# Stationary weights by chunk: all high products, then all low ones, with the low buffers moved in SBUF

## The chip, the core and the metric

The kernel runs on one core of a Trainium2 chip. The metric is the device time of one execution in microseconds (us). Engines are named as the profile names them: PE (TensorE matmuls), PEld (TensorE weight loads), DVE (VectorE), ACT (ScalarE), POOL (GpSimd), SP (SyncE, which issues most DMAs).

## What is computed

Two encoder layers on 256 tokens of width 2048, in fp32. Layer 0 mixes with gated linear attention, layer 1 with grouped-query attention and axial rotary positions. Each layer then has a squared-ReLU MLP of width 8192 and a gated per-layer embedding:

```python
for i in range(DEPTH):
    u = rms_norm(h, g_pre_mix[i])
    mix = gla_mixer(u, ...) if i % 2 == 0 else gqa_mixer(u, ...)
    h = h + rms_norm(mix, g_post_mix[i])
    m = squared_relu_mlp(rms_norm(h, g_pre_mlp[i]), w_mlp_up[i], w_mlp_down[i])
    h = h + rms_norm(m, g_post_mlp[i])
    gate = sigmoid(h @ w_ple_gate[i])
    h = h + rms_norm(gate * (p[i] @ w_ple_proj[i]), g_ple[i])
```

Nearly all work is large matrix products with weights that are read once from HBM.

## The kernel before

**Split numbers.** TensorE multiplies in float32r. To keep fp32 accuracy every operand is held as two float32r parts, high and low: high = the value rounded, low = value minus high. A product is then high x high + high x low + low x high.

**The weight stream.** `WeightStream` brings the weights in chunks of 128 x 2 x 512 elements (KC = 2 slices of the contraction, 512 KB). SP loads a chunk into one of four `raw` buffers (L82), ACT rounds it into one of four `whi` buffers (L91), DVE subtracts and writes one of four `wlo` buffers (L92). The buffers go round in order; `W.get()` hands the next finished pair to a matrix product and starts what can be started ahead.

**Two kinds of product.** In `gemm_a` the activations (X or H) are stationary and the weights move: per slice and token tile three matmuls of 512 columns, X high with `whi` (L294), X high with `wlo` (L295), X low with `whi` (L296). It makes the down projection `d`, the gate `g`, `v`, `q` of the attention and the output projections. `gemm_out` (L333 to L335) is its variant for the last column group. In `gemm_b` the weights are stationary: 128 x 128 blocks of `whi` with X as 512 columns (256 tokens high, 256 tokens low beside each other; L367), and blocks of `wlo` with the 256 high columns of X (L372). It makes `q` and `k` of layer 0, the output gate `og`, and the up projection `u`.

**Order in gemm_b.** A column group g has eight chunks c, and four PSUM accumulators f (128 output rows each). Per chunk there are eight (k, f) steps, and each step has one high and one low matmul. The order is high, low, high, low, ... . One chunk is different: the first of a group marked `fresh` (three in the program: q0, and the first group of each layer's u), which does eight high matmuls and then eight low ones. After the last chunk's step for an accumulator, `evac` folds it: ACT copies the right half (L409), DVE adds the left half (L410). There are five accumulator banks, so group g+1's accumulators 1, 2 and 3 take the banks of group g's 0, 1 and 2 when these are folded.

There are 40 column groups in `gemm_b`, thus 320 chunks: 256 in u, 32 in og, 32 in q and k. PE's order is that of the code; the orders of ACT and DVE are set by a scheduler when the program is built.

**Places in SBUF.** In the program as built, X begins at byte 33,920 of each partition, the four `whi` at 83,072, 87,168, 91,264 and 95,360, H at 172,160. All differ from X by multiples of 512 bytes, and so do h, the identity, PT and the low half of k and v in the attention (kvlow); a row of X or H has 2048 bytes, a weight block 512. The four `wlo` lie at 99,456, 103,552, 107,648 and 111,744, again at X's place modulo 512. Tiles behind them that are not placed so: `v`, prT and qT at 416 bytes past X's place modulo 512, `Sh` and lrT at 32, the small weights `lrw` at 160 and 416 in turn. The line `L1.tile([P, 24], F32, name="gap")` is what puts H at X's place.

Of the kernel before, what the change touches and what calls it, by code (L numbers as in the profile page):

```python
# [10 lines left out]
F32 = mybir.dt.float32  # L11
F32R = mybir.dt.float32r
# [5 lines left out]
P = 128  # L18
# [36 lines left out]
CH = KC * 512  # L55


class WeightStream:


    def __init__(self, nc, pool, nraw, nsplit):
        self.nc, self.pool, self.nraw, self.nsplit = nc, pool, nraw, nsplit
        self.chunks = []
        self.raw = {}
        self.split = {}
        self.nload = 0
        self.ndone = 0
        self.pos = 0
        self.on_load = {}
        self.todo = []  # L70
        self.dest = {}
        self.live = 0

    def add(self, ap, kt, n):
        self.chunks.append((ap, kt, n))
# [28 lines left out]
    def _split(self, lows=True):  # L104
        i = self.ndone
        _, kt, n = self.chunks[i]
        raw = self.raw.pop(i)
        m = kt * n
        if i in self.dest:
            hi, lo = self.dest[i]  # L110
            if len(hi.shape) == 3:
                self._cut(hi, lo, raw[:, :m].rearrange("p (k n) -> p k n", k=kt))
                self.split[i] = (hi, lo)
                self.ndone += 1
                return
        else:
            hi = self.pool.tile([P, CH], F32R, tag="whi", name=f"whi{i}", bufs=self.nsplit)
            lo = self.pool.tile([P, CH], F32R, tag="wlo", name=f"wlo{i}", bufs=self.nsplit)
            self.live += 1
        for j, k in self.parts(i):  # L120
            self._cut(hi[:, j * n:k * n], lo[:, j * n:k * n], raw[:, j * n:k * n])
        if lows:
            self.lows()
        self.split[i] = (hi[:, :m].rearrange("p (k n) -> p k n", k=kt),
                         lo[:, :m].rearrange("p (k n) -> p k n", k=kt))
        self.ndone += 1
# [24 lines left out]
def kernel(ctx, tc, a, out):  # L151
# [9 lines left out]
    def acc(name):  # L161
        return psa.tile([P, 512], F32, tag="acc", name=name)
# [192 lines left out]
    def gemm_b(op, ngroups, evac, name="b", fresh=False):  # L355
        nch = 16 // KC
        for g in range(ngroups):
            ps = [acc(f"{name}_{g}_{f}") for f in range(4)]
            for c in range(nch):
                hi, lo = W.get()  # L360
                order = [(k, f) for f in range(4) for k in range(KC)]
                if fresh and g == 0 and c < nch - 1:
                    order = [(k, f) for k in range(KC) for f in range(4)]

                def high(k, f):
                    K = c * KC + k
                    mm(ps[f], hi[:, k, f * P:(f + 1) * P], op[:, K, :], start=K == 0, stop=K == 15,  # L367
                       skip_group_check=True)

                def low(k, f):  # L370
                    K = c * KC + k
                    mm(ps[f][:, T:], lo[:, k, f * P:(f + 1) * P], op[:, K, :T], start=False, stop=K == 15,  # L372
                       skip_group_check=True)
                if fresh and g == 0 and c == 0:
                    for k, f in order:
                        high(k, f)
                    for k, f in order:
                        low(k, f)
                else:
                    for k, f in order:  # L380
                        high(k, f)
                        low(k, f)
                        if c == nch - 1 and k == KC - 1:
                            evac(g * 4 + f, ps[f])
                yield (g, c)
# [165 lines left out]
    with tc.tile_pool(name="xs", bufs=nx) as xp:  # L551
# [51 lines left out]
        def q_part(i):  # L603
            return qk[i // 2][:, 0, (i % 2) * T:(i % 2 + 1) * T]
        drive(gemm_b(X, 1, lambda i, ps: fold(ps, f"q0{i}", dst=q_part(i)), name="q0", fresh=True),
              {c - 2: [xsplit(c)] for c in range(2, nx)})

        def scale_q0():
            late0()
            for i in range(4):  # L610
                nc.vector.scalar_tensor_tensor(q_part(i), q_part(i), 1.0 / 16.0, R0["r"], op0=ALU.mult, op1=ALU.mult)
        drive(gemm_b(X, 1, qk_evac(0, 1), name="k0"), {nx - 2: [scale_q0]})

    with tc.tile_pool(name="core", bufs=1) as cp:
# [159 lines left out]
        def run_core(hd):  # L774
            for r in core(hd):
                Ss[hd] = r
                yield
        plan = {}
        cos = [None] * GH
        for hd in range(GH):  # L780
            g = run_core(hd)
# [15 lines left out]
            at(plan, o + 4, next_o(hd))  # L797
            at(plan, o + 6, next_o(hd))
        sl = drive(gemm_b(X, 1, qk_evac(1, 0), name="q1"), plan)
        sl = drive(gemm_b(X, 1, qk_evac(1, 1), name="k1"), plan, sl)  # L800
        sl = drive(gemm_a(X, 4, v_evac, name="v"), plan, sl)

    L1 = ctx.enter_context(tc.tile_pool(name="L1", bufs=1))
    L1.tile([P, 24], F32, name="gap")
    H = L1.tile([P, KT, 512], F32R, name="H")

    def load_PT(i):
# [121 lines left out]
    with tc.tile_pool(name="att", bufs=1) as ap_:  # L929
# [10 lines left out]
        for nm in ("attn_g_q", "attn_g_k"):  # L940
            g = ap_.tile([P, P], F32, name=nm)
# [154 lines left out]
        for g in range(4):  # L1096
            b = 8 * (g + 1) + ATT_LAG
# [80 lines left out]
```

## Time and profile before

| what | value |
|---|---|
| median of 3 runs | 2315.54 us (2314.12 to 2316.01) |
| the profiled execution | 2314.26 us |
| its span, first to last instruction | 2312.5 us |
| PE busy | 2288.3 us, 99% of the span |
| PEld busy | 1955.9 us, 85% |
| DVE busy, ACT busy | 1424.0 us (62%), 1214.8 us (53%) |

The 1.76 us between the span and the execution lie around the instructions. A matmul's row has its start and a modelled end: successive matmuls overlap in the rows, so the time that one costs is read from start to start.

### The profile page before, as it was taken

How to read it: one execution, taken by the hardware profiler on the slowest of the kernel's cores; microseconds unless marked ns; L12 is line 12 of the kernel's file. 1: busy time of each engine (PE TensorE's matmuls, PEld its weight loads, DVE VectorE, ACT ScalarE, POOL GpSimd, SP SyncE). 2: the span in 40 equal slices, each digit the busy share in tenths (PEclk: the TensorE clock that was granted, in tenths of full speed). 3: DMA queues.
4: the chain of work that ended last, by engine and by line, in shares of the span. 5: the costliest groups of instructions: out<-in, count | busy, mean ns of one | idle time of the engine just before them, and what ended most of it. 6: DMA issues, size and time to landing. Idle time of an engine off the chain costs nothing.

```text
span 2312.5 us, 31200 instructions
## 1 busy us (share of the span) xinstructions
PE 2288.3 (99%) x11924; PEld 1955.9 (85%) x11924; DVE 1424.0 (62%) x1920; ACT 1214.8 (53%) x1884; POOL 36.7 (2%) x58
## 2 busy tenths in 40 slices
PE   8989999999999999999999999999999999999998
PEld 7878888988888888888888888888888888888887
DVE  6787765664564555556667677665455455455565
ACT  6666554654453454455556565555455355355453
POOL 0000000000000000000000010000000000000000
PEclk9999999999999999999999999999999999999999
DMA  8545665665665665665565644665665666666654
GB/s 282 163 146 146 196 191 196 191 184 194 189 187 193 191 185 194 190 188 191 197 210 163 182 145 155 204 184 190 193 190 186 195 185 190 192 189 186 215 173 146
DMA packets 223783, 431.75 MB, mean 187 GB/s; under 512 B 15696, under 2 KB 16720, under 8 KB 222864
## 3 DMA queue, kind: packets, MB, share of 16 engines
q1 hardware_dynamic: 221328, 421.23, 59.1%
q10 hardware_dynamic: 2304, 8.52, 1.0%
q8 instruction: 93, 1.52, 0.3%
q14 instruction: 58, 0.48, 0.1%
HBM read 427.60 MB, written 2.10 MB: 186 GB/s over the span
## 4 chain that ended last, share of the span: by engine, by line
PE 96%; DVE 1%; ACT 1%; issue 1%; DMA 0%; POOL 0%; SPq 0%; DVEq 0%; POOLq 0%; ACTq 0%
PE u L367 21%; PE u L372 10%; PE d L295 9%; PE d L296 9%; PE d L294 9%; PE og L367 3%; PE g L296 2%; PE g L294 2%; PE g L295 2%; PE og L372 1%; PE q L296 1%; PE q L294 1%; PE q L295 1%; PE k L367 1%; PE ao L296 1%; PE ao L294 1%
## 5 line engine op out<-in xcount | busy, mean ns | idle before, releaser
L92 DVE TENSOR_TENSOR wlo<-raw,whi 128x1024 fp32r<-128x1024 f32 (+1 forms) x770 | 937.4, 1221 | 734.8 <-ACT whi L91 732.5
L91 ACT CAST whi<-raw 128x1024 fp32r<-128x1024 f32 (+1 forms) x770 | 806.7, 1051 | 859.1 <-PE d L296 338.6
L367 PE MATMUL u<-X,whi 128*128 128x512 f32 x2048 | 722.6, 399 | 0.0
L372 PE MATMUL u<-X,wlo 128*128 128x256 f32 x2048 | 572.5, 281 | 0.0
L367 PEld LDWEIGHTS u<-X,whi 128*128 128x128 f32 x2048 | 384.7, 188 | 95.1
L372 PEld LDWEIGHTS u<-X,wlo 128*128 128x128 f32 x2048 | 385.9, 189 | 0.4
L294 PE MATMUL d<-whi,H 128*128 128x512 f32 x960 | 373.6, 389 | 0.0
L295 PE MATMUL d<-wlo,H 128*128 128x512 f32 x960 | 373.5, 389 | 0.0
L296 PE MATMUL d<-whi,H 128*128 128x512 f32 x960 | 373.5, 389 | 0.0
L294 PEld LDWEIGHTS d<-whi,H 128*128 128x128 f32 x960 | 180.2, 188 | 37.6
L296 PEld LDWEIGHTS d<-whi,H 128*128 128x128 f32 x960 | 180.2, 188 | 37.4
L295 PEld LDWEIGHTS d<-wlo,H 128*128 128x128 f32 x960 | 180.2, 188 | 37.1
L367 PE MATMUL og<-X,whi 128*128 128x512 f32 x256 | 89.4, 393 | 0.0
L294 PE MATMUL g<-whi,X 128*128 128x512 f32 x192 | 75.3, 392 | 0.0
L296 PE MATMUL g<-whi,X 128*128 128x512 f32 x192 | 74.8, 389 | 0.0
L295 PE MATMUL g<-wlo,X 128*128 128x512 f32 x192 | 74.7, 389 | 0.0
L372 PE MATMUL og<-X,wlo 128*128 128x256 f32 x256 | 71.7, 280 | 0.0
L367 PEld LDWEIGHTS og<-X,whi 128*128 128x128 f32 x256 | 47.9, 187 | 10.5
L409 ACT COPY u_c<-u 128x256 f32<-128x256 f32 x128 | 47.2, 369 | 17.7 <-PE u L372 17.7
L367 PE MATMUL q<-X,whi 128*128 128x512 f32 x128 | 46.4, 414 | 6.0 <-ACT whi L91 5.3
L295 PE MATMUL v<-wlo,X 128*128 128x512 f32 x128 | 50.7, 396 | 0.8 <-DVE wlo L92 0.8
L294 PE MATMUL v<-whi,X 128*128 128x512 f32 x128 | 51.5, 402 | 0.0
(426 smaller groups left out, 2976.8 us busy)
## 6 DMA issues: line engine op xcount, KB each, us to landing
raw<-in_w_mlp_up SPq DMA_DIRECT2D x256, 512.0 KB, 3.7
raw<-in_w_mlp_down SPq DMA_DIRECT2D x256, 512.0 KB, 3.8
raw<-in_gla_w_in SPq DMA_DIRECT2D x95, 512.0 KB, 4.0
raw<-in_w_ple_gate SPq DMA_DIRECT2D x64, 512.0 KB, 4.2
raw<-in_attn_w_in SPq DMA_DIRECT2D x48, 512.0 KB, 4.0
raw<-in_gla_w_out SPq DMA_DIRECT2D x32, 512.0 KB, 4.3
raw<-in_attn_w_out SPq DMA_DIRECT2D x32, 512.0 KB, 4.2
raw<-in_w_ple_proj SPq DMA_DIRECT2D x7, 512.0 KB, 5.1
```

The source lines that it names most:

```text
L91: self.nc.scalar.copy(hi, raw)
L92: self.todo.append(lambda: self.nc.vector.tensor_sub(lo, raw, hi.bitcast(F32)))
L294: mm(ps[g][t], xh, hi[:, k], start=K == 0, stop=False)
L295: mm(ps[g][t], xh, lo[:, k], start=False, stop=False)
L296: mm(ps[g][t], xl, hi[:, k], start=False, stop=K == nk - 1)
L367: mm(ps[f], hi[:, k, f * P:(f + 1) * P], op[:, K, :], start=K == 0, stop=K == 15, skip_group_check=True)
L372: mm(ps[f][:, T:], lo[:, k, f * P:(f + 1) * P], op[:, K, :T], start=False, stop=K == 15, skip_group_check=True)
L409: nc.scalar.copy(cr[:parts], ps[:parts, T:])
```

## The change

In `gemm_b` every chunk but the last of a column group now does its eight high matmuls and then its eight low ones; before, only the first chunk of a fresh group did. The last chunk keeps high, low in turn, since its accumulators are folded one after the other.

The four low buffers get a tag each, and gaps stand between them, so that they lie 0, 64, 384 and 448 bytes past X's place modulo 512 (bytes 99,456, 103,616, 108,032 and 112,192). They are used in turn as before. All tiles behind them move by 448 bytes; the gap ahead of H grows by 64 bytes, so that H is at X's place again.

```diff
@@ WeightStream
+        self.turn = 0
@@ WeightStream._split
             hi = self.pool.tile([P, CH], F32R, tag="whi", name=f"whi{i}", bufs=self.nsplit)
-            lo = self.pool.tile([P, CH], F32R, tag="wlo", name=f"wlo{i}", bufs=self.nsplit)
+            b = self.turn % self.nsplit
+            if 0 < self.turn < self.nsplit:
+                self.pool.tile([P, (0, 16, 80, 16)[b]], F32, tag=f"gap{b}", name=f"gap{b}", bufs=1)
+            self.turn += 1
+            lo = self.pool.tile([P, CH], F32R, tag=f"wlo{b}", name=f"wlo{i}", bufs=1)
             self.live += 1
@@ gemm_b
-                if fresh and g == 0 and c == 0:
+                if c < nch - 1:
                     for k, f in order:
                         high(k, f)
                     for k, f in order:
                         low(k, f)
@@ tile_encoder_kernel
-    L1.tile([P, 24], F32, name="gap")
+    L1.tile([P, 24 + 16], F32, name="gap")
```

On PE, the first chunk of the second column group of u, second quarter of layer 0's MLP (`u1_1_0` is accumulator 0 of that group, X_86 is X, whi203 and wlo203 are the chunk's two buffers). Before:

```order
L367 MATMUL u1_1_0_5708<-X_86,whi203_5606 128x512
L372 MATMUL u1_1_0_5708<-X_86,wlo203_5607 128x256
L367 MATMUL u1_1_0_5708<-X_86,whi203_5606 128x512
L372 MATMUL u1_1_0_5708<-X_86,wlo203_5607 128x256
L367 MATMUL u1_1_1_5709<-X_86,whi203_5606 128x512
L372 MATMUL u1_1_1_5709<-X_86,wlo203_5607 128x256
L367 MATMUL u1_1_1_5709<-X_86,whi203_5606 128x512
L372 MATMUL u1_1_1_5709<-X_86,wlo203_5607 128x256
```

The same chunk on PE now (high is line 372 of the changed kernel, low line 377):

```order
L372 MATMUL u1_1_0_5711<-X_86,whi203_5609 128x512 x2
L372 MATMUL u1_1_1_5712<-X_86,whi203_5609 128x512 x2
L372 MATMUL u1_1_2_5713<-X_86,whi203_5609 128x512 x2
L372 MATMUL u1_1_3_5714<-X_86,whi203_5609 128x512 x2
L377 MATMUL u1_1_0_5711<-X_86,wlo203_5610 128x256 x2
L377 MATMUL u1_1_1_5712<-X_86,wlo203_5610 128x256 x2
L377 MATMUL u1_1_2_5713<-X_86,wlo203_5610 128x256 x2
L377 MATMUL u1_1_3_5714<-X_86,wlo203_5610 128x256 x2
```

Accumulators 1, 2 and 3 are first written two, four and six matmuls into the chunk, where before it was four, eight and twelve.

On DVE, the fold of the group before it (`u0_s` to `u3_s` are the folded accumulators u1_0_0 to u1_0_3; L854 applies the ReLU and a scale, L237 writes the low half of H). Before:

```order
L92 TENSOR_TENSOR wlo205_5651<-raw205_5566,whi205_5650 128x1024
L410 TENSOR_TENSOR u0_s_5661<-u1_0_0_5492,u0_c_5660 128x256
L410 TENSOR_TENSOR u1_s_5674<-u1_0_1_5493,u1_c_5673 128x256
L410 TENSOR_TENSOR u2_s_5687<-u1_0_2_5494,u2_c_5686 128x256
L854 SCALAR_TENSOR_TENSOR u0_s_5661<-u0_s_5661,R10_4190 128x256
L854 SCALAR_TENSOR_TENSOR u1_s_5674<-u1_s_5674,R10_4190 128x256
L854 SCALAR_TENSOR_TENSOR u2_s_5687<-u2_s_5687,R10_4190 128x256
L92 TENSOR_TENSOR wlo206_5713<-raw206_5588,whi206_5712 128x1024
```

The same place on DVE now (fold is line 415, ReLU line 859, the low split line 93):

```order
L93 TENSOR_TENSOR wlo205_5654<-raw205_5569,whi205_5653 128x1024
L415 TENSOR_TENSOR u0_s_5664<-u1_0_0_5495,u0_c_5663 128x256
L859 SCALAR_TENSOR_TENSOR u0_s_5664<-u0_s_5664,R10_4193 128x256
L415 TENSOR_TENSOR u1_s_5677<-u1_0_1_5496,u1_c_5676 128x256
L415 TENSOR_TENSOR u2_s_5690<-u1_0_2_5497,u2_c_5689 128x256
L859 SCALAR_TENSOR_TENSOR u1_s_5677<-u1_s_5677,R10_4193 128x256
L859 SCALAR_TENSOR_TENSOR u2_s_5690<-u2_s_5690,R10_4193 128x256
L93 TENSOR_TENSOR wlo206_5716<-raw206_5591,whi206_5715 128x1024
```

One ReLU step has moved ahead of the folds of accumulators 1 and 2; the low split still stands ahead of all of them. SP and POOL have the same orders as before.

## Rows read from the trace of the kernel before

**Rows 1.** The page: busy time and share, and granted clock in 40 slices.

```profile
PE 2288.3 (99%) x11924; PEld 1955.9 (85%) x11924; DVE 1424.0 (62%) x1920; ACT 1214.8 (53%) x1884; POOL 36.7 (2%) x58
...
PEclk9999999999999999999999999999999999999999
```

**Rows 2.** The page: the chain that ended last, by line.

```profile
PE u L367 21%; PE u L372 10%; PE d L295 9%; PE d L296 9%; PE d L294 9%; PE og L367 3%; PE g L296 2%; PE g L294 2%; PE g L295 2%; PE og L372 1%; PE q L296 1%; PE q L294 1%; PE q L295 1%; PE k L367 1%; PE ao L296 1%; PE ao L294 1%
```

**Rows 3.** Timeline of PE in u (start us, us, instruction): one period.

```profile
682.15 0.40 PE L367 MATMUL u<-X,whi 128*128 128x512 f32 x1
682.39 0.28 PE L372 MATMUL u<-X,wlo 128*128 128x256 f32 x1
682.51 0.40 PE L367 MATMUL u<-X,whi 128*128 128x512 f32 x1
...
683.21 0.40 PE L367 MATMUL u<-X,whi 128*128 128x512 f32 x1
```

**Rows 4.** Timeline of PE: first rows of stretches of 240 (u) and 176 (og) pairs.

```profile
600.53 0.40 PE L367 MATMUL u<-X,whi 128*128 128x512 f32 x1
...
685.33 0.40 PE L367 MATMUL u<-X,whi 128*128 128x512 f32 x1
...
259.26 0.39 PE L367 MATMUL og<-X,whi 128*128 128x512 f32 x1
...
320.27 0.39 PE L367 MATMUL og<-X,whi 128*128 128x512 f32 x1
```

**Rows 5.** Timeline of PE: layer 0's fresh chunk of u, and what follows.

```profile
417.45 2.00 PE L367 MATMUL u<-X,whi 128*128 128x512 f32 x8
419.29 1.11 PE L372 MATMUL u<-X,wlo 128*128 128x256 f32 x8
420.24 1.04 PE L418 MATMUL xt<-ident,h 128*128 128x128 f32 x8
```

**Rows 6.** Timeline of PE: 384 products of d, then 42 of gemm_out's halves.

```profile
688.16 0.40 PE L294 MATMUL d<-whi,H 128*128 128x512 f32 x1
...
775.00 0.39 PE L296 MATMUL d<-whi,H 128*128 128x512 f32 x1
...
1125.83 0.28 PE L333 MATMUL d<-X,H 128*128 128x256 f32 x1
...
1130.87 0.28 PE L517 MATMUL e<-whi,PT 128*128 128x256 f32 x1
```

**Rows 7.** Timeline of PE: products whose operands lie apart modulo 512.

```profile
54.70 3.87 PE L764 MATMUL lr<-X,lrw 128*64 128x512 f32 x16
58.41 0.39 PE L367 MATMUL q<-X,whi 128*128 128x512 f32 x1
...
142.27 0.28 PE L732 MATMUL o<-Sh,v 128*128 128x256 f32 x1
...
145.12 0.63 PE L639 MATMUL z<-lrT,wgk 96*128 96x256 f32 x4
...
1328.14 0.28 PE L1069 MATMUL op<-prT,vn 128*128 128x256 f32 x1
...
1328.84 0.60 PE L1055 MATMUL pp<-ident,pr 128*128 128x128 f32 x4
```

**Rows 8.** Waits by engine and line: us in total, times, longest us.

```profile
ACT whi L91 <- PE u L367: 312.5, 246, 1.8
...
PE q L367 <- ACT whi L91: 5.3, 1, 5.3
PE k L367 <- DVE qk_s L410: 2.3, 1, 2.3
```

**Rows 9.** Timeline of DVE and PE where a group of u ends.

```profile
641.27 1.23 DVE L92 TENSOR_TENSOR wlo<-raw,whi 128x1024 fp32r<-128x1024 f32 x1 [1.60 <-ACT whi L91]
642.41 1.08 DVE L410 TENSOR_TENSOR u_s<-u,u_c 128x256 f32<-128x256 f32 x3
...
642.93 0.40 PE L367 MATMUL u<-X,whi 128*128 128x512 f32 x1
```

## The prediction

> **What bounds the kernel now.** I read the page first. PE is busy for 99% of the span and its clock was granted in full in every slice [rows 1]. The chain that ended last lies almost wholly on matmuls, 31% of it on the two lines of `gemm_b` in u and 27% on the three of `gemm_a` in d [rows 2]. The longest waits of PE for another engine are 5 us or less each [rows 8]. ACT's casts, on the contrary, wait 312.5 us for u's high matmuls to give their buffer back [rows 8], so the weights are ready long before they are used. The time can therefore change in two ways only: by the number of matmuls, which stays, or by the time from one matmul's start to the next.
>
> So I went to the timeline and read starts. In u, three high-low pairs take 683.21 - 682.15 = 1.06 us [rows 3]. Over 240 pairs without a gap it is (685.33 - 600.53) / 240 = 353.3 ns for a pair [rows 4]. The same pair of matmuls in og takes (320.27 - 259.26) / 176 = 346.6 ns [rows 4], with the same shapes, operands, buffers and clock. So the alternating order has two paces, and most of u is in the slower one. The high matmul is what differs: in u it runs 240 ns to the next low at 682.15 and the low 120 ns [rows 3], then the shares shift, and after three pairs the pattern is back. Counted by the starts of the chunks, 234 of the 280 chunks that are not last in their group go at the slow pace (210 in u, 3 in og, 21 in q and k), 43 at the fast one, and 3 are fresh chunks.
>
> **The change, part by part.**
>
> *The new order.* The trace holds it already: the fresh chunk. In layer 0's u, eight highs take 419.29 - 417.45 = 1.84 us and eight lows 420.24 - 419.29 = 0.95 us [rows 5]; the fresh chunk of layer 1 has the same two durations. That is 2.79 / 8 = 348.75 ns for a pair. It also follows a run of 256-column products (e), as each chunk will now follow the lows of the one before. Two long runs give the other end: 512-column products one after the other need (775.00 - 688.16) / 383 = 226.7 ns, and 256-column ones (1130.87 - 1125.83) / 42 = 120.0 ns [rows 6], together 346.7 ns. The difference of 2 ns to the fresh chunk is the transition from one size to the other, which the long runs do not have. I take the fresh chunk, as it has the transitions:
>
> - 234 slow chunks x 8 pairs x (353.3 - 348.75) = -8.5 us
> - 43 fast chunks x 8 x (348.75 - 346.6) = +0.7 us
> - sum -7.8 us. With the long runs' 346.7 it would be 234 x 8 x 6.6 = -12.4 us.
>
> The last chunks keep their order. Into which of the two paces they fall after a run of lows no row shows; 40 x 8 x 6.7 = 2.1 us is what they hold between both. I count nothing.
>
> [...] The rows say that the same 768 columns cost 353.3 or 346.6 ns [rows 4]. [...]
>
> *The low buffers' places, in gemm_b.* Three of the four low buffers now lie apart from X modulo 512 bytes. Of the 277 chunks in the new order (without the three that had it) 208 meet such a buffer, thus 208 x 8 = 1664 low matmuls. Two kinds of 256-column product in the trace have operands that lie apart. In `o`, the weights lie 384 bytes past the moving operand, one of the new distances: (145.12 - 142.27) / 24 = 118.75 ns [rows 7]. In `op`, with 0 and 96 bytes in turn, (1328.84 - 1328.14) / 6 = 116.7 ns [rows 7]. Both are faster than the aligned 120.0 [rows 6]. I take `o`, the nearest: 1664 x -1.25 = -2.1 us; the ends are 0 and 1664 x -3.3 = -5.5 us.
>
> *The low buffers' places, in gemm_a.* There `wlo` is the moving operand of 1664 matmuls (L295), three quarters of them, 1248, now out of place against the weights that load meanwhile. The only 512-column product with operands apart is `lr`: (58.41 - 54.70) / 16 = 231.9 ns, 5.2 ns more than d's 226.7 [rows 6, 7], but its weights are 64 columns wide, not 128, and lie 160 and 416 bytes off. `o` has the right width and one of the right distances, but half the columns. I take `o`, since the load of the weights is what could collide: 1248 x -1.25 = -1.6 us. The ends: -3.3 ns as in `op`, -4.1 us, and +5.2 ns as in `lr`, +6.5 us if only these matmuls are hit. If all three products of such a chunk are, it is a rival (below).
>
> *Waits.* PSUM: a group's accumulators 1, 2 and 3 are now first written after 2, 4 and 6 highs, 0.45, 0.91 and 1.36 us from the chunk's start at 226.7 ns each, where it was 0.71, 1.41 and 2.12 us at 353.3 ns a pair. A group of u begins at 642.93 us; DVE's three folds of the group before run from 642.41 to 643.49 [rows 9]. The second and third fold move back behind one ReLU step, a third of a microsecond as the folds are. So the fold of accumulator 0 is done at about 642.8 and is wanted at 643.38, that of 1 at 643.5 and wanted at 643.84, that of 2 at 643.8 and wanted at 644.29. Nothing waits, with some 0.3 us to spare; the low split ahead of the folds (641.27) starts earlier besides, as it waits for ACT's cast, and the cast waits for the highs, which now end 0.9 us sooner in a chunk. If that spare time is gone, each of 36 group changes pays some tenths, 5 us at 0.15 us each.
>
> At the first chunk of k's second half the wait is there already: PE waits 2.3 us for a fold [rows 8] that stands behind the work of the linear attention on DVE. PE comes to it 0.24 us earlier (after two highs, not after two pairs), and one 512-wide product of DVE and two activations of ACT now stand ahead of the folds there: +1.0 us, between +0.2 and +1.5.
>
> The lows are used 1.8 us later in a chunk than before and highs at the same place, so supply only gains time. High buffers come free sooner, lows at the chunk's end as before. The tiles behind the low buffers move by 448 bytes; `o` keeps its distance of 384, the others (some 200 matmuls of the two attentions) are under 1 us at 5 ns each.
>
> **Sum.** -7.8 - 2.1 - 1.6 + 1.0 = -10.5 us. The profiled execution of 2314.26 us would take 2303.8 us. The median of the runs, 2315.54, lies 1.3 us above the profiled one; so 2305.0 us is the forecast for the median.
>
> **The rivals.**
>
> *The steadier pace.* Highs and lows settle at once and the moved lows help as in `op`: -12.4 - 5.5 - 4.1 + 1.0 = -21.0 us, 2294.5 us. For it: the fresh chunk's lows are at 119 ns already. Against it: its highs, 230 ns, are not at 226.7 [rows 5, 6].
>
> *Order is worth nothing.* PE's pace is set by something that order does not touch (columns, or the loads of the weights), and both terms vanish: 2315.5 us. For it: og reaches 346.6 ns in the old order [rows 4], so whoever runs slow may do so in the new one as well. Against it: the fresh chunks, both.
>
> *Slower.* In `gemm_a` a moved `wlo` throws the chunk out of its even 226.7 ns, all three products of it, at the pace of `lr`: 3 x 1248 x 5.2 = +19.5 us, against -8.9 us of the rest (-7.8 - 2.1 + 1.0): 2326.1 us. It decides from 8.9 / 3744 = 2.4 ns a product. For it: u shows that one stretch of aligned matmuls can fall into a slower pattern and stay there for 85 us [rows 4]. Against it: `o` and `op` do not slow down [rows 7]. Half of it, only the moved matmuls at the pace of `lr`, gives 2315.5 - 8.9 + 6.5 = 2313.1 us, no change that could be told.
>
> [...]
>
> **How the numbers follow.** The forecast, with what lies around it (2300 to 2310), 47%. The steadier pace, 17%. Order without worth, 12%. Only the moved matmuls slower, 8%. All of `gemm_a` slower, 16%. A measurement of this kernel tells about 0.2%, 4.6 us, from no change: faster is below 2310.9 (47 + 17 = 64%), no change 12 + 8 = 20%, slower 16%. The range reaches from 2291 us (the steadier pace, and 3 us for last chunks that go fast) to 2318 us, where the slow case has only begun; it leaves out most of that case and a little below. The likeliest case's own range is 2300 to 2310 us.
>
> **What the changed profile would show.** In u, a chunk as one row of eight highs and one of eight lows, 1.81 to 1.84 and 0.94 to 0.96 us from start to start; at 1.89 the order has brought nothing. In d, 226.7 ns from product to product also at the moved `wlo`; 230 or more would be the slow rival. No row of PE in u or og that waits for DVE's fold; the wait in k between 2.5 and 3.8 us. The forecast is wrong if d's pace moves by over 2 ns either way, since 4992 matmuls hang on it, or if the lows come out below 113 ns.

## The result, and the profile after

| what | before | after |
|---|---|---|
| median | 2314.83 us (2313.92 to 2316.01, 4 runs) | 2326.99 us (2324.36 to 2329.43, 4 runs) |
| the profiled execution, its span | 2314.26 us, 2312.5 us | 2324.36 us, 2322.5 us |

The ratio is 1.0052 [1.0035, 1.0069]: the change makes the kernel slower by 12.2 us. The forecast was 2305.0 us, with a range that ended at 2318. The case that came nearest is the slower rival (2326.1 us).

The page after, busy time, granted clock and the chain by line:

```profile
PE 2299.4 (99%) x11924; PEld 1955.3 (84%) x11924; DVE 1432.3 (62%) x1920; ACT 1215.6 (52%) x1884; POOL 37.7 (2%) x58
...
PEclk9999999999999999999999999999999999999999
...
PE u L372 20%; PE u L377 10%; PE d L300 10%; PE d L299 10%; PE d L301 10%; PE og L372 3%; PE g L300 2%; PE g L299 2%; PE g L301 2%; PE og L377 1%; PE q L299 1%; PE q L301 1%; PE q L300 1%; PE k L372 1%; PE go L300 1%; PE ao L299 1%
```

PE is still the bound, with the same number of matmuls and the clock granted in full (0.998 in the mean of the execution), as in [rows 1]. Against [rows 2] the share of u has gone down by one point, and each of the three lines of d has gone up by one. All three grew, not only L300, whose moving operand is the low block. The timeline of PE, one quarter of u and the quarter of d behind it:

```profile
599.77 2.02 PE L372 MATMUL u<-X,whi 128*128 128x512 f32 x8
601.63 1.11 PE L377 MATMUL u<-X,wlo 128*128 128x256 f32 x8
602.58 1.99 PE L372 MATMUL u<-X,whi 128*128 128x512 f32 x8
...
689.06 0.40 PE L299 MATMUL d<-whi,H 128*128 128x512 f32 x1
689.29 0.40 PE L300 MATMUL d<-wlo,H 128*128 128x512 f32 x1
689.53 0.39 PE L301 MATMUL d<-whi,H 128*128 128x512 f32 x1
689.76 0.40 PE L299 MATMUL d<-whi,H 128*128 128x512 f32 x1
...
777.76 1.09 PE L372 MATMUL u<-X,whi 128*128 128x512 f32 x4
```

In u, eight highs and eight lows take 602.58 - 599.77 = 2.81 us here, and the 256 pairs of the quarter (777.76 belongs to the next one) take (689.06 - 599.77) / 256 = 348.8 ns each, where [rows 4] gave 353.3. In d, 384 products take (777.76 - 689.06) / 384 = 231.0 ns each, where [rows 6] gave 226.7. That is where the time went. A slice is one of the two parts of a weight chunk along the contraction, taken for one token tile: three products in `gemm_a`. Read over the whole trace from start to start, leaving out the 34 of 1664 slices and some 17 of 320 chunks that have a pause or other work inside:

- the three products of a slice in `gemm_a`: 681.4 ns before, 692.8 ns after; 1664 x 11.4 = +19.0 us
- a chunk of `gemm_b`: 2819.3 ns before, 2793.6 ns after; 320 x -25.7 = -8.2 us
- together +10.8 us, of the span's +10.0

PE's waits after, in us, times and the longest:

```profile
PE q L372 <- ACT whi L92: 5.1, 1, 5.1
...
PE k L372 <- DVE qk_s L415: 2.4, 1, 2.4
...
PE k L372 <- DVE qk L415: 0.2, 1, 0.2
```

No wait took part: these are as in [rows 8], and no row of u or og waits for a fold.

### The profile page after: what moved, and what is told of

Its sections match the earlier page's. It is cut to its first block, busy times and chain, and to the rows that moved or that the text cites. A ratio compares the mean times of both kernels' runs of the same rounds, so it can differ in the third digit from the quotient of the medians.

```text
span 2322.5 us, 31219 instructions
## 1 busy us (share of the span) xinstructions
PE 2299.4 (99%) x11924; PEld 1955.3 (84%) x11924; DVE 1432.3 (62%) x1920; ACT 1215.6 (52%) x1884; POOL 37.7 (2%) x58
## 4 chain that ended last, share of the span: by engine, by line
PE 96%; DVE 1%; ACT 1%; issue 1%; DMA 0%; POOL 0%; SPq 0%; DVEq 0%; POOLq 0%; ACTq 0%
PE u L372 20%; PE u L377 10%; PE d L300 10%; PE d L299 10%; PE d L301 10%; PE og L372 3%; PE g L300 2%; PE g L299 2%; PE g L301 2%; PE og L377 1%; PE q L299 1%; PE q L301 1%; PE q L300 1%; PE k L372 1%; PE go L300 1%; PE ao L299 1%
## 5 line engine op out<-in xcount | busy, mean ns | idle before, releaser
L372 PE MATMUL u<-X,whi 128*128 128x512 f32 x2048 | 540.0, 393 | 0.0
L372 PEld LDWEIGHTS u<-X,whi 128*128 128x128 f32 x2048 | 369.2, 188 | 69.7
L300 PE MATMUL d<-wlo,H 128*128 128x512 f32 x960 | 377.6, 393 | 0.0
L377 PE MATMUL u<-X,wlo 128*128 128x256 f32 x2048 | 320.5, 281 | 0.0
L377 PEld LDWEIGHTS u<-X,wlo 128*128 128x128 f32 x2048 | 292.2, 188 | 18.2
L300 PEld LDWEIGHTS d<-wlo,H 128*128 128x128 f32 x960 | 180.2, 188 | 40.8
L300 PE MATMUL g<-wlo,X 128*128 128x512 f32 x192 | 75.5, 393 | 0.0
L372 PE MATMUL og<-X,whi 128*128 128x512 f32 x256 | 67.8, 394 | 0.0
L415 DVE TENSOR_TENSOR u_s<-u,u_c 128x256 f32<-128x256 f32 x128 | 53.7, 420 | 1.1 <-ACT u_c L414 0.4
L861 ACT ACTIVATE sq<-u_s 128x256 f32<-128x256 f32 x128 | 52.6, 417 | 0.5 <-DVE u_s L859 0.5
L241 ACT CAST H<-sq 128x256 fp32r<-128x256 f32 x128 | 51.0, 404 | 1.7
L859 DVE SCALAR_TENSOR_TENSOR u_s<-u_s,R 128x256 f32<-128x256 f32 x128 | 51.1, 420 | 1.2
```

The costliest lines, as they stand in the source:

```text
L241: nc.scalar.copy(dst_hi, src)
L300: mm(ps[g][t], xh, lo[:, k], start=False, stop=False)
L415: nc.vector.tensor_add(s[:parts], ps[:parts, :T], cr[:parts])
L859: nc.vector.scalar_tensor_tensor(s, s, 0.0, RM["r"], op0=ALU.max, op1=ALU.mult)
L861: nc.scalar.activation(s2, s, AF.Square)
```

## The experiments

Theory after the result: the order gains what was forecast, and the low buffers' places cost `gemm_a` all three products. Rivals: the new order leaves `gemm_a` in a bad pattern; or only the mixture of four places costs, not a place. Ten kernels were run; each median is over 4 to 11 executions, and each ratio is to executions of before taken beside them. In each diff, lines with - are those of the kernel named in the sentence ahead of it. "Three products" and "chunk" are means from start to start over a trace, as above; places are bytes past X's place modulo 512 ("four" stands for 0, 64, 384 and 448 in turn).

| run | order in gemm_b | high, low at | three products, ns | chunk, ns | median us | ratio to before |
|---|---|---|---|---|---|---|
| before | old | 0, 0 | 681.4 | 2819 | | 1 |
| after | new | 0, four | 692.8 | 2794 | 2326.99 | 1.0052 [1.0035, 1.0069] |
| order_only | new | 0, 0 | 681.2 | 2796 | 2307.10 | 0.9970 [0.9958, 0.9982] |
| place_only | old | 0, four | 692.8 | 2793 | 2324.96 | 1.0044 [1.0031, 1.0057] |
| order_all64 | new | 0, 64 | 696.0 | 2782 | 2325.89 | 1.0048 [1.0036, 1.0061] |
| order_all448 | new | 0, 448 | 687.3 | 2787 | 2315.66 | 1.0005 [0.9996, 1.0013] |
| both64 | new | 64, 64 | 687.0 | 2781 | 2313.45 | 0.9991 [0.9982, 1.0000] |
| shift_all64 | new | 0, 0 (all moved) | 681.1 | 2796 | 2307.12 | 0.9965 [0.9953, 0.9978] |
| hi64 | new | 64, 0 | 699.7 | 2809 | 2343.07 | 1.0118 [1.0104, 1.0132] |
| both448 | new | 448, 448 | 700.0 | 2772 | 2328.46 | 1.0059 [1.0046, 1.0073] |
| by_use_alt | old | 0, 64 in gemm_b, 0 in gemm_a | 681.4 | 2774 | 2301.46 | 0.9939 [0.9925, 0.9952] |
| by_use_order | new | 0, 64 in gemm_b, 0 in gemm_a | 681.4 | 2781 | 2304.15 | 0.9954 [0.9942, 0.9967] |

**order_only**: the order alone, on the kernel before.

```diff
-                if fresh and g == 0 and c == 0:
+                if c < nch - 1:
```

> The new order in gemm_b, all four low buffers at X's place as before. Theory (displaced low buffers slow all three products of gemm_a, the order itself gains): d back at 226.7 ns a product, a chunk of u at about 2.79 us where it was 2.83, 8 us less than before, about 2307 us. Rival (the new order hands gemm_a over in a bad pattern, and the places are innocent): d stays at 231 ns, 2320 us or more.

The timeline of PE of this run, the same quarter:

```profile
596.83 1.98 PE L367 MATMUL u<-X,whi 128*128 128x512 f32 x8
598.64 1.12 PE L372 MATMUL u<-X,wlo 128*128 128x256 f32 x8
599.60 2.00 PE L367 MATMUL u<-X,whi 128*128 128x512 f32 x8
...
686.29 0.40 PE L294 MATMUL d<-whi,H 128*128 128x512 f32 x1
...
773.34 0.39 PE L367 MATMUL u<-X,whi 128*128 128x512 f32 x1
```

d is at (773.34 - 686.29) / 384 = 226.7 ns, to the digit that of [rows 6]; u is at (686.29 - 596.83) / 256 = 349.5 ns a pair. The median is 7.6 us under that of before in the same rounds (2314.70). So the order gains, and it does nothing to `gemm_a`.

**place_only**: the places alone, on the kernel after.

```diff
-                if c < nch - 1:
+                if fresh and g == 0 and c == 0:
```

> The old alternating order, low buffers at 0, 64, 384 and 448 bytes. Theory: gemm_a as in the changed kernel, 692.9 ns for three products where it was 681.4, +19 us; u stays near 353 ns a pair, so about 2334 us. Rival (the order did it): d at 226.7 ns and 2315 us.

Timeline of PE, the same quarter:

```profile
600.51 0.39 PE L372 MATMUL u<-X,whi 128*128 128x512 f32 x1
600.74 0.28 PE L377 MATMUL u<-X,wlo 128*128 128x256 f32 x1
600.86 0.39 PE L372 MATMUL u<-X,whi 128*128 128x512 f32 x1
...
689.90 0.40 PE L299 MATMUL d<-whi,H 128*128 128x512 f32 x1
...
778.58 0.39 PE L372 MATMUL u<-X,whi 128*128 128x512 f32 x1
```

d is at 88.68 / 384 = 230.9 ns in the old order too, so the rival that the order spoils `gemm_a` falls. What I had not reckoned with is u: (689.90 - 600.51) / 256 = 349.2 ns a pair. The places alone take `gemm_b` out of its slow pace, by as much as the order alone (2793 against 2796 ns a chunk), and both together bring no more (2794). The two edits share one gain.

**order_all64, order_all448**: all four low buffers at one place, on the kernel after (for 448 the gap ahead of the first low buffer is 112 elements, and that ahead of H stays at 24 + 16).

```diff
-            if 0 < self.turn < self.nsplit:
-                self.pool.tile([P, (0, 16, 80, 16)[b]], F32, tag=f"gap{b}", name=f"gap{b}", bufs=1)
+            if self.turn == 0:
+                self.pool.tile([P, 16], F32, tag="gap", name="gapw", bufs=1)
...
-    L1.tile([P, 24 + 16], F32, name="gap")
+    L1.tile([P, 24 + 112], F32, name="gap")
```

> New order, all four low buffers 64 bytes past X's place. Theory (what counts is how far the moving low buffer lies from the weights that load): three products 694 ns in every chunk of gemm_a, +21 us there and -9 us in gemm_b, about 2327 us. Rival (only the mixture of four places hurts, since the pattern never settles): d at 226.7 ns, about 2306 us.

> New order, all four low buffers 448 bytes past X's place. Theory: three products 690 ns, +14 us in gemm_a, -9 us in gemm_b, about 2320 us. Rival (mixture): d at 226.7 ns, about 2306 us.

Timeline of PE with all low buffers at 64:

```profile
690.59 0.40 PE L299 MATMUL d<-whi,H 128*128 128x512 f32 x1
690.83 0.39 PE L300 MATMUL d<-wlo,H 128*128 128x512 f32 x1
691.06 0.40 PE L301 MATMUL d<-whi,H 128*128 128x512 f32 x1
691.29 0.39 PE L299 MATMUL d<-whi,H 128*128 128x512 f32 x1
...
779.67 0.40 PE L372 MATMUL u<-X,whi 128*128 128x512 f32 x1
```

89.08 / 384 = 232.0 ns: the single place 64 costs more than the mixture, so the rival of the mixture falls. The three products take 231.5, 232.1 and 232.4 ns in the mean. The high blocks did not move, and their products are hit as much as the low one. At 448 the cost is 6 ns a slice instead of 15, less than the 9 ns and the 2320 us that I had expected there. Sorted by what runs beside them, order_all64's slices take 696.4 ns where DVE is at rest (under 5% busy, 250 slices) and 695.6 where it is over 80% busy (738); for ACT it is 696.0 ns both at rest (548) and over 80% busy (424). No slice has both engines at rest. So neither engine's work shows in the pace.

**both64, shift_all64**: on order_only, high and low buffers moved together; and X, raw, high, low and H all moved together.

```diff
 both64
+            if not self.split and self.ndone == 0:
+                self.pool.tile([P, 16], F32, tag="gapw", name="gapw", bufs=1)
             hi = self.pool.tile([P, CH], F32R, tag="whi", name=f"whi{i}", bufs=self.nsplit)
...
-    L1.tile([P, 24], F32, name="gap")
+    L1.tile([P, 24 + 112], F32, name="gap")
 shift_all64
+    base.tile([P, 16], F32, name="gapx")
```

> New order as in the order-only run, with all four low buffers and all four high buffers of the weights 64 bytes past X's place modulo 512; X and H themselves stay. Theory 1: what costs is that the moving buffer lies elsewhere modulo 512 than the stationary rows that PEld reads beside it. Then the three products of a slice take at least as long as with the low buffers alone at 64 (696 us per thousand, thus 696 ns), since now all three moving blocks are displaced: 1664 times at least 15 ns over the order-only run's 681.2, a median of 2326 us or more. Theory 2: what costs is the change of place from one product to the next (high block, low block, high block). Then this run, in which high and low blocks share a place, is back at 681 ns, and the median lies at 2300 to 2308 us.

> New order as in the order-only run, with X, the raw, high and low weight buffers and H all moved on by 64 bytes together, so that their places relative to each other modulo 512 are those of the order-only run; h and the identity are not moved. Theory 1: only the place of moving and stationary operand relative to each other counts. Then the three products stay at 681 ns, a gemm_b chunk at 2796 ns, and the median at 2307 us (2305.5 to 2309). Theory 2: the absolute place modulo 512 counts. Then the products of gemm_a go towards the 696 ns of the run with the low buffers at 64, and the median towards 2326 us.

Timeline of PE with everything moved together:

```profile
597.38 0.39 PE L368 MATMUL u<-X,whi 128*128 128x512 f32 x1
...
686.83 0.40 PE L295 MATMUL d<-whi,H 128*128 128x512 f32 x1
...
773.88 0.39 PE L368 MATMUL u<-X,whi 128*128 128x512 f32 x1
```

d is at 87.05 / 384 = 226.7 ns, u at 349.4 ns a pair, the median at 2307.12: as order_only in everything. A move of X, raw, high, low and H by the same 64 bytes changed nothing: the places that counted here are those relative to each other. With both blocks at 64, neither theory held: 687.0 ns lies between the 696 of the one and the 681 of the other. Moving the high blocks after the low ones gives back 9 of the 15 ns.

**hi64, both448**: the high buffers alone at 64, and all eight at 448, as in both64 but for the gaps (112 ahead of the high buffers for both448; for hi64 another 112 ahead of the low ones).

```diff
 hi64, on both64
+            if not self.split and self.ndone == 0:
+                self.pool.tile([P, 112], F32, tag="gapl", name="gapl", bufs=1)
             lo = self.pool.tile([P, CH], F32R, tag="wlo", name=f"wlo{i}", bufs=self.nsplit)
...
-    L1.tile([P, 24 + 112], F32, name="gap")
+    L1.tile([P, 24], F32, name="gap")
 both448, on both64
-                self.pool.tile([P, 16], F32, tag="gapw", name="gapw", bufs=1)
+                self.pool.tile([P, 112], F32, tag="gapw", name="gapw", bufs=1)
...
-    L1.tile([P, 24 + 112], F32, name="gap")
+    L1.tile([P, 24 + 16], F32, name="gap")
```

> New order, only the four high buffers 64 bytes past X's place modulo 512; low buffers, X and H at X's place. In gemm_a two of three moving blocks are displaced against the stationary rows, and the low block lies 64 bytes below its high one. Theory: two shares, one for high and low lying apart (with low 64 below high that share was 6 ns in the run with low at 448) and one for both lying off X's place (6 ns in the run with both at 64), which add up: three products take 693 ns, 1664 times 12 ns = 20 us over the order-only run, about 2326 us. Rival: what counts is only the place of the low block against the high one; then 687 ns and 2316 us.

> New order, high and low buffers all at 448 bytes past X's place modulo 512 (64 below the next multiple). Theory: the share of both blocks lying off X's place does not depend on the side: three products take 687 ns as with both at 64, and the median is 2313 us if gemm_b's chunks are at 2781 to 2787 ns. Rival: the share depends on the side, as that of the low block alone did (15 ns at 64, 6 ns at 448): then the three products take 681 to 684 ns or over 690, and the median is below 2309 or above 2318 us.

Timeline of PE with the high buffers alone at 64:

```profile
693.04 0.39 PE L298 MATMUL d<-whi,H 128*128 128x512 f32 x1
...
782.63 0.40 PE L371 MATMUL u<-X,whi 128*128 128x512 f32 x1
```

89.59 / 384 = 233.3 ns, and 2343.07 us, the slowest kernel of all: two shares that add up (693 ns) are not the rule, and the place of the low block against the high one is not either. The tiles behind the low buffers lie in hi64 where they lie in before, modulo 512, so it is not their move that costs. With both at 448 it is 700.0 ns, and 687.0 with both at 64, so the side matters, as its rival said. I found no simple rule for the sizes.

**by_use_alt, by_use_order**: low blocks at 64 where `gemm_b` loads them as weights, at 0 where `gemm_a` moves them; on before, and on order_only. The scores' buffer S has one copy instead of two, to make room.

```diff
-            lo = self.pool.tile([P, CH], F32R, tag="wlo", name=f"wlo{i}", bufs=self.nsplit)
+            o = self.shift.get(i, 0)
+            lo = self.pool.tile([P, CH + 128], F32R, tag="wlo", name=f"wlo{i}", bufs=self.nsplit)[:, o:o + CH]
...
-            wchunks(a["w_mlp_up"][i], q * 2048, 2048)
+            wchunks(a["w_mlp_up"][i], q * 2048, 2048, o=16)
```

> Old order (high, low in turn). Low blocks that gemm_b uses as stationary weights lie 64 bytes past X's place modulo 512, low blocks that gemm_a moves lie at X's place; both are cut out of the same four buffers. The scores' buffer S has one copy in place of two to make room. Theory: place costs in gemm_a and gains in gemm_b, each by itself. Then the three products of gemm_a are at 681 ns as before, a gemm_b chunk at 2775 ns in place of 2819 (the places-only run's chunks at 64), thus 320 times 44 ns = 14 us less than before: 2301 us (2299 to 2304). Rival: the gain of the places-only run's chunks comes from the change of place from chunk to chunk and not from the place itself; then a gemm_b chunk stays near 2819 ns and the median at 2313 to 2316 us.

> The same placing by use (gemm_b's low blocks at 64, gemm_a's at 0), with the new order. Theory: place and order in gemm_b don't add up, but the run with all low buffers at 64 and the new order had 2782 ns a chunk against 2796 at place 0, so this run has 681 ns for gemm_a's three products, 2782 ns for a gemm_b chunk, and 2302.5 us (2300 to 2305), 4 to 5 us below the order-only run and a little above or at the old order with the same placing. Rival: with gemm_a's products at 0 between them the new order adds to the place: 2775 less 23, 2752 ns a chunk, 2293 us.

Timeline of PE in the old order, low blocks placed by use:

```profile
596.90 0.39 PE L371 MATMUL u<-X,whi 128*128 128x512 f32 x1
597.13 0.28 PE L376 MATMUL u<-X,wlo 128*128 128x256 f32 x1
597.25 0.40 PE L371 MATMUL u<-X,whi 128*128 128x512 f32 x1
...
685.65 0.40 PE L298 MATMUL d<-whi,H 128*128 128x512 f32 x1
...
772.74 0.39 PE L371 MATMUL u<-X,whi 128*128 128x512 f32 x1
```

Here u is at (685.65 - 596.90) / 256 = 346.7 ns a pair and d at 87.09 / 384 = 226.8: both at the best pace that [rows 4, 6] show. 2301.46 us is as expected, and beats before by 13.9 us. The chunks alone account for that (320 x -45.6 ns = -14.6 us), so the single copy of S is not what gained. With the new order on top:

```profile
597.17 1.98 PE L371 MATMUL u<-X,whi 128*128 128x512 f32 x8
598.98 1.11 PE L376 MATMUL u<-X,wlo 128*128 128x256 f32 x8
599.92 0.63 PE L371 MATMUL u<-X,whi 128*128 128x512 f32 x2
...
686.17 0.40 PE L298 MATMUL d<-whi,H 128*128 128x512 f32 x1
```

u is at (686.17 - 597.17) / 256 = 347.7 ns, and the median at 2304.15, 2.7 us above the old order in the same rounds. Order and place do not add up; once the place is right, the new order costs a little. The first eight highs and lows take 2.75 us here against 2.77 in order_only.

## Why the prediction was wrong

- **The bound** was read rightly: pace of matmuls, few waits (the longest was 5.3 us [rows 8], not "5 us or less").
- **The new order, -7.8 us**: right. Order_only gained 7.6 us (span: 2312.5 - 2304.9). The price from the fresh chunk [rows 5], 348.75 ns a pair, against 349.5 over the quarter of order_only, which has the last chunks in it.
- **Low places in gemm_b, -2.1 us**: of little worth beside the new order (2794 against 2796 ns a chunk, -0.8 us); within its ends, but as the mean of four places (with all at 64 a chunk takes 2782 ns, with all at 448 2787). That places alone would gain as much as the order (320 x -26.6 = -8.5 us in place_only) stood in no step: I had priced the place only by lows of other products, and what changes in the old order is u's hi-to-low step, 236.2 ns in the mean before and 231.9 in place_only, while low to high stays at 117.
- **Low places in gemm_a, -1.6 us: the step that failed.** Measured +19.0 us. I had two rows, `o` (width of the weights, 256 columns, and, as I read it, one of the distances) and `lr` (512 columns, other distances and width) [rows 7], and chose `o`, "since the load of the weights is what could collide". But `o` had none of `gemm_a`'s distances: in `o` the weights lie 384 bytes past the moving operand, whereas in `gemm_a` the moving low block lies 64, 384 or 448 bytes past the weights, and the side counts (696 ns at 64, 687 at 448, which is 64 on the other side). `lr`'s 231.9 ns was nearer the truth: order_all64's d is at 232.0, though this closeness is partly luck, as `lr`'s distances and width are those of no run. The second half of the error is the count: 1248 moved matmuls, where all three products of a slice pay. The slower rival had both, and 2326.1 us; its chance of 16% was the misjudgement. Its sizes are not quite those of the runs: it has 15.6 ns for each of 1248 slices, where these pay 12.4, and the other 416, whose low block is at place 0, pay 8.8 as well (below). That it came within 1 us is partly luck. The sign of being wrong that the prediction named for d (over 2 ns either way) did come: 231.0 against 226.7 ns.
- **The argument against the slower rival**, that `o` and `op` do not slow down [rows 7], did not carry over to `gemm_a`: the same three products took 681 to 700 ns there, by place. Where the time is lost no run shows.
- **The wait in k, +1.0 us**: 2.4 + 0.2 against 2.3 us [rows 8], +0.3, at the low end of what was stated.
- **No wait for folds, supply no worse**: right.

The account of the 22.0 us between forecast and result: gemm_a 19.0 + 1.6 = 20.6; gemm_b 9.9 - 8.2 = 1.7; the wait -0.7; the median 2.6 us above the profiled execution instead of 1.3, +1.3; the rest, -0.9, is not assigned.

That the places cause the loss in `gemm_a` is shown by runs that have one edit without the other, and so is that either edit alone brings the whole gain of the change in `gemm_b`. Why a place costs what it does stays open.

## What to carry to other kernels

Where a buffer is used in two roles (here as loaded weights and as moving operand), price a move of it in each role by itself, and place it by use: that gave 2301.5 us, where one place for all four low buffers gave 2307 at best of those run. Of two rows near an unknown cost, do not let a guess at the mechanism choose; when 5000 instructions hang on it and the rows have opposite signs, give both a real chance. And two edits that healed the same slow pace did not add up here (a chunk of `gemm_b` from 2819 ns to 2796 by the order alone, to 2793 by the places alone, to 2794 by both): try each alone first.

## What the runs showed of the hardware

The pace of `gemm_a`'s 512-column float32r products, with a weight load each, depended in these runs on where their operands lie modulo 512 bytes relative to each other: for (high, low) at (0, 0), (64, 64), (0, 448), (0, 64), (64, 0), (448, 448) three products took 681, 687, 687, 696, 700 and 700 ns, at a granted clock of 0.996 to 0.998. That 512 is a period fits by_use_alt, whose low buffers lie 4608 bytes apart, not 4096: its slices take the 681.4 ns of before. Whether a shorter period would do as well no run shows.

The changed kernel adds (0, 384). The buffers are used in turn, so its d in the quarter of the first timeline (from 689.06) begins with a chunk whose low block is at place 384. First products of its last three slices, and of the next chunk:

```profile
689.76 0.40 PE L299 MATMUL d<-whi,H 128*128 128x512 f32 x1
...
690.46 0.40 PE L299 MATMUL d<-whi,H 128*128 128x512 f32 x1
...
691.16 0.40 PE L299 MATMUL d<-whi,H 128*128 128x512 f32 x1
...
691.86 0.40 PE L299 MATMUL d<-whi,H 128*128 128x512 f32 x1
```

They take 0.70 us each. Over the whole trace the last of a chunk's four slices takes 681.0, 696.2, 699.3 and 687.8 ns at 0, 64, 384 and 448: in the mixture, each of the places 0, 64 and 448 comes near the pace that it has in the runs with one place alone (681, 696, 687).

And in the changed kernel a chunk's pace depended on what ran before it. The timeline of PE in d of the changed kernel, first product of each slice of a chunk whose low block is at place 0:

```profile
694.62 0.39 PE L299 MATMUL d<-whi,H 128*128 128x512 f32 x1
...
695.32 0.39 PE L299 MATMUL d<-whi,H 128*128 128x512 f32 x1
...
696.01 0.39 PE L299 MATMUL d<-whi,H 128*128 128x512 f32 x1
...
696.70 0.39 PE L299 MATMUL d<-whi,H 128*128 128x512 f32 x1
...
697.38 0.39 PE L299 MATMUL d<-whi,H 128*128 128x512 f32 x1
```

The four slices take 0.70, 0.69, 0.69 and 0.68 us; over the whole trace 698.2, 690.9, 691.3 and 681.0 ns. This chunk has the places of the kernel before, and only its fourth slice has that kernel's pace again. So the slices at place 0 took 690.2 ns in the mean, and a quarter of the buffers left in place saved little. What keeps the earlier pace for so long no run shows.
